# Gate and up of a SwiGLU by Strassen's seven products for four pairs of blocks, operands at low addresses

## The chip, the cores and the metric

The kernel runs on one core of a Trainium2 chip. The metric is the device time of one execution in microseconds (us). Its engines work at the same time and each takes its own instructions in the order in which they stand: PE (TensorE) multiplies matrices, DVE (VectorE) and ACT (ScalarE) work element by element, POOL (GpSimd) does a little arithmetic and issues DMAs, SP (SyncE) only issues DMAs. SBUF is the memory on the chip from which the engines read, PSUM the one into which PE accumulates, in eight banks of 128 x 512 float32 here.

## The reference

The program is a decoder trunk of two layers on `x` of 512 tokens by 1024 channels, all in float32:

```python
_, S, _ = x.shape          # 512 tokens, D_MODEL = 1024, D_FF = 2816
# layer 0: pooling mixer; layer 1: differential attention; after each mixer:
x = layernorm(ALPHA * x + mixer(x))
x = layernorm(ALPHA * x + swiglu(x))

def _swiglu(x, w_gate, w_up, w_down):
    return (jax.nn.silu(x @ w_gate) * (x @ w_up)) @ w_down
```

The change concerns the two SwiGLU blocks. Each has `gate` and `up`, 512 x 1024 by 1024 x 2816, and `down`, 512 x 2816 by 2816 x 1024.

## The kernel before

Every float32 operand of a product is held as two tiles of a matmul type: a high part, which an ACT cast makes, and a low part, which DVE makes by subtracting the high part from the original. A product is three matmuls, high by high, high by low and low by high (`mm3`, lines 106 to 110). The order on each engine is that of the program text; nothing reorders it.

**Gate and up.** The 2816 hidden columns are 22 blocks of 128 (`FB` = 22, `HALF` = 11). For each block and for each of gate and up there are 8 steps over the 1024 channels with 3 matmuls each, 24 matmuls of 128 x 128 weights by 512 tokens, into one PSUM bank. The first three blocks of layer 0 and the first two of layer 1 (`early`) are done in two halves of 256 tokens, since the second half of x comes later; the others run in the loop at lines 587 to 606. The blocks are taken in the order 0, 11, 1, 12, ..., so two consecutive ones form a pair k of hidden rows k and k+11. A weight tile of 128 x 1024 comes by a DMA on SP's queue (`raw`, four buffers, `RAWS`), is cast by ACT (line 89), and DVE makes the low part (line 90); there are six buffers for such pairs (`WBUFS`). After a block, ACT takes Silu of the gate (line 459) and DVE multiplies it with up (line 460), which gives a row of `hid`.

**Down** is already done by seven products in Winograd's form of Strassen's method, in the order P1, Q5, P6, Q3, P7, P2, Q4 (`DOWN`); each has 66 matmuls, 33 for each of two token blocks (line 629). What these products need as sums is made while gate and up run. `sum_weights` (line 474) loads four blocks of the weights of `down`, makes four sums on DVE (line 484) and stores them into DRAM (`tsum`) from POOL's queue. `sum_hidden` (line 491), after each pair of rows, makes sums of rows of `hid`: a copy of the first quarter to `a11` (ACT line 497, DVE line 499), three DVE operations of 256 columns (lines 498, 500 to 504), an ACT cast (line 505), and later the low part (line 508) and a store into `ssum`. While `down` runs, `r` tiles are loaded from the weights or from `tsum`, cast and subtracted (`dh`, `dl`), and the left operands come from `a11`, from `hid` or from `ssum`.

**Order around the change.** Six weights are prepared ahead. PE waits for a weight's low part and for its high part, ACT's cast waits for the DMA and for a free buffer, which PE frees when the product that used it is done. The affine part of the layer norm (lines 189, 190) and the loads of its parameters stand among the early blocks.

Of the kernel before, what the change touches and what calls it, by code (L numbers as in the profile page):

```python
# [50 lines left out]
def trunk(ctx, tc, x, wall, pscale, lam_p, subln, table, lng, lnb, band, first, onehot, out):  # L51
# [8 lines left out]

    res = keep.tile([P, SB, D], F32, name="res")
# [30 lines left out]
    def ready(upto, low=None):  # L92
        while divided[0] < min(upto, total):
            c = divided[0]
            fetch(c + RAWS)
            h = keep.tile([P, 1024], F32R, tag="wh", name=f"wh{c}", bufs=WBUFS)
            l = keep.tile([P, 1024], F32R, tag="wl", name=f"wl{c}", bufs=WBUFS)
            split(h, l, raws.pop(c), low=low)
            parts[c] = (h, l)
            divided[0] += 1  # L100
# [20 lines left out]


    xt = keep.tile([P, 2, 2, KB, 256], F32R, name="xt")
# [93 lines left out]
    with tc.tile_pool(name="pool", bufs=1) as pp:  # L217
# [52 lines left out]
        ph = pp.tile([P, KB, S], F32R, name="ph")  # L270
        pl = pp.tile([P, KB, S], F32R, name="pl")
# [13 lines left out]
        def pool_weights(c):  # L285
            h = keep.tile([P, 1024], F32R, tag="wh", name=f"pwh{c}", bufs=WBUFS)
            l = keep.tile([P, 1024], F32R, tag="wl", name=f"pwl{c}", bufs=WBUFS)
# [145 lines left out]

    ROWS = [slice(k, k + n) for k, n in PAIRS]

    def ffn(layer, late):
        n = 2 * layer + 1
        final = n == 2 * DEPTH - 1
        c0 = base[0]
        with tc.tile_pool(name=f"ffn{layer}", bufs=1) as fp:  # L440


            hid = fp.tile([P, FB, S], F32, name=f"hid{layer}")
            a11 = fp.tile([P, 2, HALF, 256], F32R, name=f"a11_{layer}")

            def product(acc, c, lo, hi):
                h, l = weights(c)
# [9 lines left out]
            def gated(f, pg, pu):  # L457
                sg = keep.tile([P, S], F32, tag="y", name=f"sg{layer}_{f}", bufs=2)
                nc.scalar.activation(sg, pg, AF.Silu)  # L459
                nc.vector.tensor_tensor(hid[:, f, :], sg, pu, op=ALU.mult)  # L460

            c1 = c0 + 2 * FB

            order = [k + j * HALF for k in range(HALF) for j in range(2)]
            tsum = dram.tile([4, len(PAIRS), P, 1024], F32, name=f"tsum{layer}")
            ssum = dram.tile([P, 2, 2, HALF, 256], F32, name=f"ssum{layer}")

            def block(i, b):

                if PAIRS[i][1] == 2:  # L470
                    return wall[c1 + 4 * i + b]
                return wall[c1 + 20 + b // 2][:, (b % 2) * 512 : (b % 2 + 1) * 512]

            def sum_weights(k):

                i, j = k // 2, k % 2
                c = slice(j * 512, (j + 1) * 512)
                b11, b12, b21, b22 = t = [
                    fp.tile([P, 512], F32, tag=f"b{b}", name=f"b{b}_{layer}_{k}") for b in range(4)
                ]  # L480
                for b in range(4):
                    nc.sync.dma_start(out=t[b], in_=block(i, b)[:, c])
                for z, x, y in ((b11, b11, b12), (b12, b12, b22), (b22, b11, b22), (b21, b22, b21)):
                    nc.vector.tensor_tensor(z, x, y, op=ALU.add)  # L484
                for m, z in enumerate((b11, b22, b12, b21)):
                    nc.gpsimd.dma_start(out=tsum[m, i, :, c], in_=z)

            late_low = []
            summed_rows = [0]

            def sum_hidden(k):
                first, second = hid[:, k, :256], hid[:, k, 256:]
                a12, a22 = hid[:, k + HALF, :256], hid[:, k + HALF, 256:]
                u = fp.tile([P, 2, 256], F32, tag="u", name=f"u{layer}_{k}", bufs=1)
                v = fp.tile([P, 2, 2, 256], F32R, tag="v", name=f"v{layer}_{k}", bufs=1)
                tt = nc.vector.tensor_tensor
# [16 lines left out]
            def settle():  # L513
                while late_low:
                    late_low.pop(0)()
# [587 lines left out]
```

## Time and profile before

Three runs took 980.78, 982.01 and 984.98 us, median 982.01 us.

| | us |
|---|---|
| profiled execution | 983.17 |
| its span in the trace | 981.1 |
| PE busy | 963.2 (98%) |
| DVE busy | 643.4 (66%) |
| ACT busy | 420.5 (43%) |
| POOL busy | 123.7 (13%) |

By stage, in us from the start of the span: pooling mixer 0 to 41, gate and up of layer 0 from 41 to 284, its down to 391, a turn to 406.6, attention to 570.5, its output product to 635, gate and up of layer 1 to 864, its down to 953.3, the tail to 981.1.

In rows of the page, "x66" counts instructions, "us, mean ns" are the busy time of a group and the duration of one. Matmuls overlap, so the time between the starts of two is less than a matmul's own duration. A row in a timeline is a start, a busy time and what ran, with "[idle <- engine]" for a wait ahead of it.

### The profile page before, as it was taken

The numbers are of one execution on the slowest core, as the hardware profiler recorded it, in microseconds if no ns is written. First come the engines' busy times: TensorE is split into PE (matmuls) and PEld (weight loads), VectorE is DVE, ScalarE is ACT, GpSimd is POOL, SyncE is SP. The second block draws the span as 40 slices with busy tenths as digits, with TensorE's granted clock in tenths as the row PEclk, the third lists the DMA queues.
The fourth block names the chain that finished last, engine by engine and source line by source line (L and its number), as shares of the span: only waits on it lengthen the run. The fifth ranks groups of instructions, "written<-read, shape, count | busy, mean of one in ns | idle before, by whom it ended". The sixth has DMA issues, their size and how long they took to land.

```text
span 981.1 us, 13416 instructions
## 1 busy us (share of the span) xinstructions
PE 963.2 (98%) x4974; PEld 820.6 (84%) x4974; DVE 643.4 (66%) x1007; ACT 420.5 (43%) x708; POOL 123.7 (13%) x195
## 2 busy tenths in 40 slices
PE   8999999999999999999999999999999999999995
PEld 8898888888888888988888888988888888888884
DVE  6845874455567577688777676756655555477687
ACT  5753222223326357656556554732223322244460
POOL 4201111111120211000000000011111111111102
PEclk9999999999999999999999999999999999999997
DMA  8247768655776984323222122276665566878942
GB/s 223 66 158 247 250 228 289 229 193 193 266 257 236 329 295 151 114 82 94 73 87 86 55 86 86 90 270 211 225 256 193 209 229 228 288 246 297 341 145 86
DMA packets 70079, 188.59 MB, mean 192 GB/s; under 512 B 15956, under 2 KB 16084, under 8 KB 70014
## 3 DMA queue, kind: packets, MB, share of 16 engines
q1 hardware_dynamic: 56588, 141.57, 42.1%
q0 software_dynamic: 13408, 46.15, 13.9%
q8 instruction: 39, 0.64, 0.3%
q14 instruction: 26, 0.21, 0.1%
q10 hardware_dynamic: 18, 0.02, 0.0%
HBM read 150.99 MB, written 36.72 MB: 191 GB/s over the span
## 4 chain that ended last, share of the span: by engine, by line
PE 94%; DVE 3%; ACT 1%; POOL 1%; issue 0%; POOLq 0%; DVEq 0%
PE P L629 13%; PE g L109 8%; PE u L108 8%; PE u L109 8%; PE g L108 8%; PE u L110 8%; PE g L110 8%; PE Q L629 6%; PE s L814 2%; PE v L108 2%; PE v L110 2%; PE v L109 2%; PE wo L108 2%; PE wo L109 2%; PE wo L110 2%; PE q L109 1%
## 5 line engine op out<-in xcount | busy, mean ns | idle before, releaser
L90 DVE TENSOR_TENSOR wl<-raw,wh 128x1024 fp32r<-128x1024 f32 x118 | 141.7, 1220 | 33.3 <-ACT wh L89 33.3
L89 ACT CAST wh<-raw 128x1024 fp32r<-128x1024 f32 x120 | 123.5, 1050 | 65.9 <-PE u L109 63.9
L109 PE MATMUL g<-xt,wh 128*128 128x512 f32 (+1 forms) x392 | 144.1, 368 | 0.5 <-DVE xt L90 0.5
L108 PE MATMUL g<-xt,wh 128*128 128x512 f32 (+1 forms) x392 | 144.3, 368 | 0.0
L108 PE MATMUL u<-xt,wh 128*128 128x512 f32 (+1 forms) x392 | 144.1, 368 | 0.0
L110 PE MATMUL u<-xt,wl 128*128 128x512 f32 (+1 forms) x392 | 144.0, 367 | 0.0
L109 PE MATMUL u<-xt,wh 128*128 128x512 f32 (+1 forms) x392 | 144.0, 367 | 0.0
L110 PE MATMUL g<-xt,wl 128*128 128x512 f32 (+1 forms) x392 | 144.0, 367 | 0.0
L460 DVE TENSOR_TENSOR hid<-sg,u 128x512 f32<-128x512 f32 x44 | 30.3, 688 | 154.9 <-PE u L110 154.5
L90 DVE TENSOR_TENSOR dl<-r,dh 128x1024 fp32r<-128x1024 f32 x84 | 94.3, 1132 | 38.8 <-ACT dh L89 38.7
L89 ACT CAST dh<-r 128x1024 fp32r<-128x1024 f32 x84 | 81.5, 979 | 69.6 <-PE P L629 31.7
L629 PE MATMUL P<-dh,xt 128*128 128x512 f32 x352 | 109.4, 390 | 0.0
L109 PEld LDWEIGHTS g<-xt,wh 128*128 128x128 f32 x392 | 73.9, 189 | 12.7 <-DVE xt L90 0.7
L110 PEld LDWEIGHTS u<-xt,wl 128*128 128x128 f32 x392 | 73.9, 189 | 12.3
L108 PEld LDWEIGHTS u<-xt,wh 128*128 128x128 f32 x392 | 73.9, 189 | 12.1
L110 PEld LDWEIGHTS g<-xt,wl 128*128 128x128 f32 x392 | 73.9, 188 | 12.2
L108 PEld LDWEIGHTS g<-xt,wh 128*128 128x128 f32 x392 | 73.9, 188 | 12.2
L109 PEld LDWEIGHTS u<-xt,wh 128*128 128x128 f32 x392 | 73.9, 188 | 12.0
L505 ACT CAST v<-u 128x512 fp32r<-128x512 f32 x22 | 13.7, 621 | 159.4 <-issue 142.5
L629 PEld LDWEIGHTS P<-dh,xt 128*128 128x128 f32 x352 | 66.1, 188 | 13.6
L484 DVE TENSOR_TENSOR b<-b,b 128x512 f32<-128x512 f32 x88 | 60.8, 691 | 18.4 <-DMA b<-in_wall 16.2
L459 ACT ACTIVATE sg<-g 128x512 f32<-128x512 f32 x44 | 26.3, 599 | 103.5 <-PE g L110 102.0
(189 smaller groups left out, 1792.5 us busy)
## 6 DMA issues: line engine op xcount, KB each, us to landing
raw<-in_wall SPq DMA_DIRECT2D x128, 512.0 KB, 4.2
b<-in_wall SPq DMA_DIRECT2D x88, 256.0 KB, 5.6
tsum<-b POOLq DMA_DIRECT2D x88, 256.0 KB, 4.7
r<-tsum SPq DMA_DIRECT2D x40, 512.0 KB, 4.7
r<-in_wall SPq DMA_DIRECT2D x30, 512.0 KB, 5.0
ssum<-v POOLq DMA_DIRECT2D x22, 512.0 KB, 4.0
xt<-ssum POOLq DMA_DIRECT2D x20, 512.0 KB, 6.0
res<-in_x SPq DMA_DIRECT2D x8, 256.0 KB, 6.4
```

The lines of the kernel that those rows point to most:

```text
L89: nc.scalar.copy(dst_h, src)
L90: (low or nc.vector).tensor_tensor(dst_l, src, dst_h.bitcast(F32), op=ALU.subtract)
L108: nc.tensor.matmul(acc, ah, bh, start=start, stop=False)
L109: nc.tensor.matmul(acc, ah, bl, start=False, stop=False)
L110: nc.tensor.matmul(acc, al, bh, start=False, stop=stop)
L459: nc.scalar.activation(sg, pg, AF.Silu)
L460: nc.vector.tensor_tensor(hid[:, f, :], sg, pu, op=ALU.mult)
L484: nc.vector.tensor_tensor(z, x, y, op=ALU.add)
L505: nc.scalar.copy(v[:, :, 0, :], u)
L629: nc.tensor.matmul(accs[s], x[:, k, r], y[:, c], start=first and k == 0 and e == 0, stop=last and k == m - 1 and e == 2, skip_group_check= ...
L814: nc.tensor.matmul(accs[c][:, :wide], a[r, qs], b[r, :wide], start=i == 0, stop=i == 2)
```

## The change

1. **Seven products for four pairs.** For the pairs 4, 6, 7 and 9 of hidden rows (`SPLIT`), in both layers, gate and up are done by `strassen(k)`: x is cut into two halves of tokens by two halves of channels, the weights into two halves of channels by gate and up. Each of the seven products has 24 matmuls of 128 x 128 by 256 tokens. Three PSUM banks are used: A (products P1, P6, P7, Q4), C (Q5, Q3) and B (P2). A and C go on accumulating after they have been copied out: A after P1 (ACT, line 814) and after P6 (line 818), C after Q5 (line 816); the others are taken out by DVE (lines 820, 822, 824), with two Silus (lines 825, 828) and two products on DVE (832, 834). Seven weight tiles are made out of four by four DVE sums of 128 x 1024 (line 552), then seven casts (line 555) and seven low parts (line 558) in place of four each. The weights are laid out for it beforehand.
2. **Sums of x** (`sums_of_x`): eight DVE operations, four casts and four low parts of 128 x 1024 per layer, spread over the early blocks and blocks 3 to 5.
3. **Weight sums of down**: a row's blocks come by two POOL DMAs, a third adds two blocks onto them while it transfers; DVE adds two times 128 x 512 (lines 657, 658) per row, and ACT's queue issues the two stores. The rows of sums stand at the early blocks 0 and 1, at blocks 3, 5, 7, 11 and 17, and behind each Strassen pair.
4. **`sum_hidden`** makes no `a11`; P1 of down gets its left operand from `hid`, and P6 a subtraction (line 719). `v` has two buffers, its store is issued by ACT.
5. **Placement**: the tiles of x, a region for pooled values, sums of x and attention heads, and the weight pairs are the first in SBUF, so that these operands have low addresses.
6. `RAWS` is 5; the scratch of dynamic DMAs is 8192 bytes; the loads of the norm's parameters stand elsewhere.

```diff
-RAWS = 4
+RAWS = 5
+SPLIT = (4, 6, 7, 9)
+GATE = ("P1", "Q5", "P6", "Q3", "P7", "P2", "Q4")
...
+    xt = keep.tile([P, 2, 2, KB, 256], F32R, name="xt")
+    def region(name):
+        return keep.tile([P, 8192], F32R, tag="region", name=name)
...
+                if k in SPLIT:
+                    chunks += [(c, ()), (c, (c, c + 1)), (c, (c, c + 2)), (c + 2, ())]
+                    chunks += [(c + 1, (c + 1, c + 2)), (c + 3, ()), (c, (c, c + 3))]
+                    step("cast", j0)
+                    for w in (
+                        "low 0, sum 1, cast 1, sum 4, cast 3, cast 4, low 1, sum 2, cast 2, low 3, "
+                        "low 2, sum 6, cast 5, cast 6, low 4, low 5, low 6"
+                    ).split(", "):
...
+                    if kind == "sum":
+                        tt(t, raws[pair[0]], raws[pair[1]], op=ALU.add)
+                    elif kind == "cast":
+                        halves[j] = weight_pair(f"g{layer}_{j}")
+                        nc.scalar.copy(halves[j][0], t)
+                    else:
+                        h, l = halves[j]
+                        tt(l, t, h.bitcast(F32), op=ALU.subtract)
...
+                for j in range(2):
+                    nc.gpsimd.dma_start(out=t[:, j], in_=src[:, j])
+                nc.gpsimd.dma_start(out=t[:, 0], in_=src[:, :, 1], accum_op=ALU.add)
...
+            def sum_terms(k):
+                t = terms.pop(k)
+                tt(t[:, 1, 1], t[:, 0, 0], t[:, 1, 1], op=ALU.add)
+                tt(t[:, 1, 0], t[:, 1, 1], t[:, 1, 0], op=ALU.add)
+                yield
...
+                for j in range(2):
+                    nc.scalar.dma_start(out=dst[:, j], in_=t[:, j])
...
             def sum_hidden(k):
...
-                nc.scalar.copy(a11[:, 0, k, :], first)
+                tt(u[:, 0, :], first, second, op=ALU.subtract)
                 tt(second, second, a22, op=ALU.subtract)
...
+                tt(u[:, 1, :], a12, first, op=ALU.subtract)
+                tt(u[:, 1, :], u[:, 1, :], second, op=ALU.add)
                 nc.scalar.copy(v[:, :, 0, :], u)
+                yield
+                tt(v[:, :, 1, :], u, v[:, :, 0, :].bitcast(F32), op=ALU.subtract)
+                yield
+                nc.scalar.dma_start(out=ssum[:, :, :, k, :], in_=v.bitcast(F32))
...
+            def strassen(k):
+                names = {"P1": "A", "P6": "A", "P7": "A", "Q4": "A", "Q5": "C", "Q3": "C", "P2": "B"}
...
+                for j, p in enumerate(GATE):
+                    acc = banks[names[p]]
+                    h, l = halves[index[k] + j]
+                    xh, xl = lefts[p]
+                    for f in range(2):
+                        o = acc[:, f * 256 : (f + 1) * 256]
+                        for kk in range(4):
+                            c = slice((4 * f + kk) * P, (4 * f + kk + 1) * P)
+                            for e, (w, x) in enumerate(((h, xh), (h, xl), (l, xh))):
+                                nc.tensor.matmul(
+                                    o, w[:, c], x[:, kk, :],
...
+                    if p == "P1":
+                        g0 = tile_of(0)
+                        nc.scalar.copy(both(g0), acc)
+                    elif p == "Q5":
+                        nc.scalar.copy(second, acc)
+                    elif p == "P6":
+                        nc.scalar.copy(first, acc)
+                    elif p == "Q3":
+                        tt(first, acc, first, op=ALU.subtract)
...
+                    ahead(index[k] + j + 6)
+                    catch_up()
...
+                weight_sums()
+                behind.append(sum_hidden(k))
```

`catch_up` runs the next piece of each unfinished `sum_terms` and `sum_hidden` (up to its next `yield`); `ahead` prepares weights up to the sixth product ahead.

The order on ACT in layer 0 between the blocks 13 and 16 (pairs 6 and 7), first before. The names `wh` and `g_..h` are high parts of weights, `sg` a Silu, `v` the sums of hidden rows, `a` the copy to a11.

```order
L459 ACTIVATE sg_17_1809<-g_13_1747 128x512
L497 CAST a_0_534<-hid_533 128x256
L505 CAST v_6_1813<-u_6_1812 128x2x256
L89 CAST wh_1849<-raw_1738 128x1024
L89 CAST wh_1897<-raw_1773 128x1024
L459 ACTIVATE sg_7_1901<-g_14_1821 128x512
L89 CAST wh_1932<-raw_1803 128x1024
```

The same place in the changed kernel: the second half of pair 6 is behind, pair 7 begins (A_7 and C_7 are its PSUM banks).

```order
L828 ACTIVATE sg_6_1_1961<-A_6_1727 128x512
L555 CAST g_39h<-raw_1804 128x1024
L555 CAST g_40h<-raw_1578 128x1024
L814 COPY sg_7_0_2001<-A_7_1974 128x512
L662 DMA tsum_536<-b_7_1612 128x2x512 x2
L687 CAST v_6_2013<-u_6_2012 128x2x256
L816 COPY hid_534<-C_7_1975 128x2x256
L555 CAST g_41h<-raw_1836 128x1024
L818 COPY hid_534<-A_7_1974 128x2x256
```

The copies out of the banks A_7 and C_7 stand in ACT's queue behind two stores and behind the cast of `v`, which was followed by weight casts alone before.

DVE at the same place, before; `wl` and `g_..l` are low parts of weights, `b` weight sums of down, `u` and `v` sums of hidden rows.

```order
L460 TENSOR_TENSOR hid_533<-sg_17_1809,u_13_1748 128x512
L498 TENSOR_TENSOR hid_533<-hid_533 128x256
L499 TENSOR_TENSOR a_0_534<-hid_533,a_0_534 128x256
L500 TENSOR_TENSOR hid_533<-hid_533 128x256
L501 SCALAR_TENSOR_TENSOR u_6_1812<-hid_533 128x256
L504 TENSOR_TENSOR u_6_1812<-hid_533 128x256
L90 TENSOR_TENSOR wl_1850<-raw_1738,wh_1849 128x1024
L508 TENSOR_TENSOR v_6_1813<-u_6_1812,v_6_1813 128x2x256
```

DVE in the changed kernel from P2 of pair 6 to the sums of its hidden rows:

```order
L824 TENSOR_TENSOR sg_6_0_1754<-B_6_1729,sg_6_0_1754 128x512
L832 TENSOR_TENSOR hid_534<-sg_6_0_1754,hid_534 128x2x256
L552 TENSOR_TENSOR raw_1578<-raw_1578,raw_1804 128x1024
L558 TENSOR_TENSOR g_38l<-raw_1694,g_38h 128x1024
L834 TENSOR_TENSOR hid_534<-sg_6_1_1961,hid_534 128x2x256
L657 TENSOR_TENSOR b_7_1612<-b_7_1612 128x512
L658 TENSOR_TENSOR b_7_1612<-b_7_1612 128x512
L558 TENSOR_TENSOR g_39l<-raw_1804,g_39h 128x1024
L683 TENSOR_TENSOR u_6_2012<-hid_534 128x256
L684 TENSOR_TENSOR hid_534<-hid_534 128x256
L685 TENSOR_TENSOR u_6_2012<-hid_534 128x256
L686 TENSOR_TENSOR u_6_2012<-u_6_2012,hid_534 128x256
```

Ahead of the rows of `u` there now stand weight sums, low parts and evacuations of PSUM of the pair itself, and the two weight sums of down.

More of the change, by code (lines that the diff above doesn't have):

```diff
@@ L459, in gated @@
                 nc.scalar.activation(sg, pg, AF.Silu)
[L460 to L486, printed above, removed]
@@ L609, in ffn @@
+            f = early
+            while f < FB:
+                if f // 2 in SPLIT:
+                    strassen(f // 2)
+                    f += 2
+                else:
+                    plain(f)
+                    f += 1
+            load_gb(n)
+            while behind:
+                catch_up()
             fetched[0] = divided[0] = c1 + FB
@@ L723, in scalars @@
                 )
+            whole = region("heads").rearrange("p (h i t) -> p h i t", h=HEADS, i=2)
+            slots = {h: whole[:, h] for h in range(HEADS)}
+            rest = xt[:, 1].rearrange("p i k t -> p (i k t)").rearrange("p (h i t) -> p h i t", h=4, i=2)
+            slots.update({16 + h: rest[:, h - 6] for h in (6, 7)})
             where = [base[0]]
```

350 lines of the change are left out of this document (251 added, 99 removed).

## The prediction

> **What bounds the kernel now.** I read the page's busy times and its chain of waits first, then the table of stretches, then the timeline of PE for the time from one matmul to the next.
>
> ```profile
> PE 963.2 (98%) x4974; PEld 820.6 (84%) x4974; DVE 643.4 (66%) x1007; ACT 420.5 (43%) x708; POOL 123.7 (13%) x195
> ...
> PE 94%; DVE 3%; ACT 1%; POOL 1%; issue 0%; POOLq 0%; DVEq 0%
> ```
>
> ```profile
> 41.00:284.00 243.00, 243.00 (x1216) 207.42 (x1217) 137.83 (x190) 78.16 (x114) 31.46 (x55) 1.00 0.66 225
> 284.00:391.00 107.00, 107.00 (x479) 88.10 (x477) 78.85 (x101) 58.40 (x85) 14.73 (x22) 1.00 0.73 253
> 635.00:864.00 229.00, 229.00 (x1055) 191.49 (x1054) 127.34 (x176) 64.39 (x86) 29.70 (x53) 1.00 0.67 234
> 864.00:953.30 89.30, 89.30 (x394) 73.66 (x393) 64.85 (x80) 46.04 (x59) 10.31 (x15) 1.00 0.76 268
> ```
>
> The columns are the stretch, its length, busy us of PE, weight loads, DVE, ACT and POOL, PE's granted clock, DMA share and GB/s. In gate and up and in down of both layers PE is busy for the whole stretch at clock 1.00, and it makes up 94% of the chain. So the time of these stretches is the number of matmuls by the time between their starts: taking matmuls away shortens it in full, and anything else counts only where it makes PE wait. DVE has 243.00 − 137.83 = 105 us free in the first gate and up, and 229.00 − 127.34 = 102 in the second; ACT has more.
>
> **Step 1, the matmuls.** Of the two shapes:
>
> ```profile
> 299.45 14.97 PE Q L629 x66
> ```
>
> ```profile
> 41.97 0.28 PE L108 MATMUL g<-xt,wh 128*128 128x256 f32 x1
> ...
> 44.97 0.28 PE L109 MATMUL u<-xt,wh 128*128 128x256 f32 x1
> ```
>
> The first row, of the chain, is one product of down: 66 matmuls of 512 columns in 14.97 us, 226.8 ns each. The other two, of PE's timeline, have 24 rows between them: 25 matmuls of 256 columns in 44.97 − 41.97 = 3.00 us, 120.0 ns each. A pair of blocks was 4 x 24 = 96 matmuls of 512: 96 x 226.8 = 21.77 us. It becomes 7 x 24 = 168 of 256: 168 x 120.0 = 20.16 us, 2.88 per product. That is −1.61 a pair and −12.9 for the eight pairs. One multiplication in eight goes (12.5%), but only 7.4% of the time, since two matmuls of 256 columns take 13 ns more than one of 512.
>
> By the Trainium skill ("TensorE: Matmul & The Clock Gate", section "Back-to-back issue gap") a lone matmul costs columns / 2.4 GHz plus about 2.5 ns, 215.8 and 109.2 ns, by which this step would be an estimated −19.0 us. The same section gives 81 ns at 128 and 131 ns at 512 columns as what is sustained between matmuls that each load weights; between these, 256 columns come to about 98 ns, and the step would be an estimated +31 us, a loss. The rows decide against both, as this trace has both shapes, each with a weight load per matmul.
>
> **Step 2, the addresses.** Two places of the trace are slower per matmul of 512 columns than the rest:
>
> ```profile
> 284.10 15.35 PE P L629 x66
> ...
> 863.72 15.35 PE P L629 x66
> 879.07 14.97 PE Q L629 x66
> ```
>
> ```profile
> 595.78 0.39 PE L109 MATMUL wo<-wl,oh 128*128 128x512 f32 x1
> ...
> 598.12 0.39 PE L110 MATMUL wo<-wh,ol 128*128 128x512 f32 x1
> ```
>
> P1 of down takes 15.35 us in both layers, 0.38 more than Q5: 232.6 ns a matmul. Attention's output product takes (598.12 − 595.78) / 10 = 234 ns (nine rows lie between). The first reads `a11`, the second `oh` and `ol`; both tiles lie at the high end of SBUF in the program before, and the change puts their replacements low. If it is the address, the gain is 2 x 0.38 = 0.8 us for P1 and 192 x (234 − 227) = 1.3 for the 192 matmuls of that product, of which those of heads 6 and 7 read a third tile: I take −1.9 in all. Bounds: 0 (it is something else) and −2.1. The Trainium skill ("SBUF — State Buffer", section "Who interferes with whom") has PE wait for no one, which makes this part nothing; the 0.38 us of the rows above speaks for some cost of place, and whether it is the place only the run tells.
>
> **Step 3, the new waits.** The copies out of PSUM are in the order of ACT's queue, and PE has one product (2.88 us) between the end of Q5 and the start of Q3, which goes on accumulating in C. Line 816 must be done by then. It stands behind the cast of `v`, which needs the four DVE operations of 256 columns of the hidden sums, and these stand behind whatever DVE is late with. The prices:
>
> ```profile
> L90 DVE TENSOR_TENSOR wl<-raw,wh 128x1024 fp32r<-128x1024 f32 x118 | 141.7, 1220 | 33.3 <-ACT wh L89 33.3
> L460 DVE TENSOR_TENSOR hid<-sg,u 128x512 f32<-128x512 f32 x44 | 30.3, 688 | 154.9 <-PE u L110 154.5
> L616 DVE SCALAR_TENSOR_TENSOR res<-res,P 128x512 f32<-128x512 f32 x20 | 13.4, 682 | 3.2 <-PE P L629 3.2
> L498 DVE TENSOR_TENSOR hid<-hid 128x256 f32<-128x256 f32 x22 | 9.3, 424 | 0.7
> ```
>
> ```profile
> L89 ACT CAST wh<-raw 128x1024 fp32r<-128x1024 f32 x120 | 123.5, 1050 | 65.9 <-PE u L109 63.9 <-issue 1.3 <-ACT line L422 0.7
> L505 ACT CAST v<-u 128x512 fp32r<-128x512 f32 x22 | 13.7, 621 | 159.4 <-issue 142.5 <-DVE u L504 16.9
> L89 ACT CAST kh<-k 128x512 fp32r<-128x512 f32 x8 | 4.7, 587 | 26.1 <-PE k L110 26.1
> ```
>
> ```profile
> 104.84 2.35 DVE L90 TENSOR_TENSOR wl<-raw,wh 128x1024 fp32r<-128x1024 f32 x2
> 110.12 0.69 DVE L460 TENSOR_TENSOR hid<-sg,u 128x512 f32<-128x512 f32 x1 [2.93 <-PE u L110]
> 110.84 0.42 DVE L498 TENSOR_TENSOR hid<-hid 128x256 f32<-128x256 f32 x1
> ...
> 112.78 1.22 DVE L189 TENSOR_TENSOR res<-res,gb 128x1024 f32<-128x1024 f32 x1
> ```
>
> ```profile
> 109.85 0.39 PE L108 MATMUL g<-xt,wh 128*128 128x512 f32 x1
> ```
>
> Neighbours overlap a little: two of 1024 columns take 2.35 (so the second adds 1.13), five of 256 take 112.78 − 110.84 = 1.94, 0.39 each. From the first matmul of the next product (109.85) to DVE's start on the finished bank (110.12) pass 0.27 us.
>
> A pair that follows plain blocks (4, 6, 9; t = 0 is its first matmul): DVE starts the last Silu product at 0.27 and has it, two weight sums, one weight sum of 1024 and a low part done by 4.5. ACT copies A at 3.15 to 3.75 and casts a weight to 4.8, whose low part ends at 5.95. The four operations of `u` end at 7.6, the cast of `v` at 8.25, the copy of C at 8.85. Q3 is due at 3 x 2.88 = 8.64: PE waits about 0.25.
>
> Pair 7 follows pair 6 directly. DVE begins line 820 of pair 6 after Q3, at 4 x 2.88 + 0.25 + 0.27 = 12.05. From there to the end of the four operations of `u` stand nine of 1024 columns (1.13 to 1.22: 10.2 to 11.0 us), seven of 512 (0.60 to 0.69: 4.2 to 4.8), four of 256 (1.6) and a Silu between lines 824 and 832 that DVE waits for (0.60 and two hand-overs, 0.75): 16.8 to 18.2, so 28.9 to 30.2. The cast of `v` and the copy of C with their hand-overs are 1.4 more: 30.3 to 31.6. Q3 of pair 7 is due at 20.16 + 0.25 + 8.64 = 29.05. PE waits 1.2 to 2.6 us; I take 2.0, as most of these operations need the one before. That DVE has no pause between 12 and 30 us, though the stage as a whole has 100 us free, is the point: the free time lies in other pairs.
>
> Per layer 3 x 0.25 + 2.0 = 2.75, both layers +5.5. Bounds: 0 (no copy is late: hand-overs and prices all at their low end), and 2.6 in all eight pairs, +21, if each starts as late as pair 7.
>
> **What I cost at nothing.** The added DVE work per layer is 4 x 3 = 12 more low parts, 16 weight sums, 12 operations on x (40 x 1.13 = 45 us) and evacuations, against the 102 to 105 us free; without that cover it would be those 45 us. Weights stay up to six products (17 us) ahead, against 4.2 us for a load and 2.3 for cast and low part. The casts added are under half of ACT's free time. Moved DMAs:
>
> ```profile
> raw<-in_wall SPq DMA_DIRECT2D x128, 512.0 KB, 4.2
> b<-in_wall SPq DMA_DIRECT2D x88, 256.0 KB, 5.6
> tsum<-b POOLq DMA_DIRECT2D x88, 256.0 KB, 4.7
> ```
>
> SP loses the 88 loads of `b`, POOL the 88 stores and 22 of `v`, which ACT now issues. A row of weight sums comes by two loads and a third transfer on top of them; at the prices of the rows of `b` and `tsum` that is some 16 us if they go one after the other (5.6 + 5.6 + 4.7). They are issued two rows ahead, some 40 us, and for row 3 one row, 21.8 us (step 1). If the sum waited, DVE would stand at line 657 with the low parts of the next weights behind it, and PE behind those. The low parts added to P1 of down and the subtraction added to P6 cost DVE six operations of 512 columns in each, in stretches with 107.00 − 78.85 = 28 and 24 us free. Head and tail have the same instructions.
>
> **The sum.** −12.9 − 1.9 + 5.5 = −9.3 us on the profiled execution's own time, 983.17 (span 981.1 and 2.1 around it): 973.9. That execution lies 1.2 above the median of the runs, 982.0, on which the sum gives 972.7. I forecast 973.3.
>
> **The rivals.**
>
> *All waits hidden.* The copies come in time: for it, three of four pairs per layer are only 0.25 us over by hand, and two neighbours on DVE can overlap more than I take. Against it, pair 7's sum is over even at its low end. −12.9 − 1.9 = −14.8: 967.8.
>
> *The waits eat the gain.* DVE is the bound of a Strassen pair. A pair has 11 operations of 1024 columns (12.4 to 13.4 us), seven of 512 and the low part of `v` (4.8 to 5.5), four of 256 (1.6) and the Silu (0.75): 19.6 to 21.3 against PE's 20.16. Against it, six of eight pairs come after plain blocks of 10.9 us in which DVE has a third free. If each pair runs 1.2 to 1.6 us over, 8 x 1.4 = 11.2 instead of 5.5: 982.0 − 14.8 + 11.2 = 978.4, and with 0 for the addresses 980.3. About 980, no change.
>
> *A late chain of three transfers, slower.* POOL's accumulating transfer reads what the first wrote, its speed is in no row, and DVE waits for it in its queue at line 657. Up to 21.8 us for the three it costs nothing; from about there DVE starts its sums late behind every Strassen pair, and pair 7's upper price comes up in all eight: 8 x 2.6 = 21, 982.0 − 14.8 + 21 = 988. For it speaks that the copies stand behind it on ACT too; against it that 16 us are not 21.8, and that the DMA share is 0.67.
>
> *The change does not do what it says.* The addresses might do nothing, +1.9 on the forecast, 975.2; it stays inside the forecast's own range.
>
> **How the numbers follow.** The forecast, with part of the waits, .45; waits hidden .25; gain eaten .20; slower .10. Half a percent, 4.9 us, is about what such runs tell from no change: faster is below 977.1. The forecast's own range is 970 to 977, of which I leave .05 above. Faster: .40 + .25 + .05 of the eaten gain = .70. Same: .05 + .14 = .19, and .01 from the edge of the slower case, .20. Slower: .10. The range takes the hidden case from 966.5 and the eaten one up to 982: below it lie .05, above it .12.
>
> **What would show it.** The row of 66 for P1 of down at 14.97 (step 2). 168 matmuls of 256 columns in 20.2 us in pair 4 (step 1). Waits of PE ahead of Q3, at line 816's copy, about 0.25 in pairs 4, 6, 9 and 2.0 in pair 7 (step 3), and none elsewhere in gate and up. What would make it wrong: a spacing of 256 columns other than 120 ns with the new weights, waits for low parts instead of copies, or DVE at line 657 waiting for a DMA.

## The result and the profile after

The change took 970.01 us, median of six runs (967.32 to 971.13), against 981.89 us of the kernel before in the same sessions. The ratio is 0.9875, 95% interval 0.9854 to 0.9895: 1.25% faster, where 973.3 us and 0.9% were forecast. The profiled execution took 971.13 us, its span 969.2.

The first lines of the page of the change, busy time and the chain that ended last:

```profile
PE 950.4 (98%) x5550; PEld 838.2 (86%) x5550; DVE 722.7 (75%) x1069; ACT 462.6 (48%) x754; POOL 120.5 (12%) x151
...
PE 89%; DVE 7%; ACT 2%; issue 1%; POOL 1%; POOLq 0%; DVEq 0%; ACTq 0%
```

DVE now has 7% of the chain instead of 3%. Where it stands is seen by stage. In the next two fences the span is cut at the same places in both kernels: at the first matmul of gate and up, of down, of attention, of attention's output product, of the next gate and up and of the next down, and at the end of the last matmul. The stage of attention is left out. The columns are the stretch, its length, busy time of PE, weight loads, DVE, ACT and POOL, then PE's granted clock, DMA share and GB/s. These cuts differ from those ahead of the prediction: gate and up of layer 1 begins at 621.96 us and not at 635, and its down runs to the last matmul at 968.84. The kernel before:

```profile
40.14:283.94 243.80, 243.31 (x1219) 207.52 (x1217) 138.48 (x192) 78.98 (x116) 31.98 (x55) 1.00 0.66 225
283.94:392.26 108.32, 108.07 (x487) 89.01 (x486) 80.17 (x103) 59.66 (x86) 14.75 (x22) 1.00 0.72 250
...
570.49:621.96 51.47, 51.47 (x245) 41.97 (x243) 38.58 (x67) 25.21 (x52) 3.85 (x7) 1.00 0.25 81
621.96:863.56 241.60, 241.60 (x1164) 204.15 (x1163) 135.90 (x187) 76.80 (x110) 30.32 (x54) 1.00 0.65 227
863.56:968.84 105.28, 105.28 (x463) 86.58 (x461) 79.67 (x104) 48.21 (x63) 15.12 (x22) 1.00 0.67 237
968.84:981.10 12.26, 0.00 (x0) 0.00 (x0) 6.05 (x10) 0.00 (x0) 2.43 (x3) 0.59 0.23 86
```

The change:

```profile
40.17:279.63 239.46, 237.68 (x1506) 216.27 (x1505) 176.56 (x217) 99.46 (x137) 32.33 (x37) 1.00 0.78 249
279.63:387.40 107.77, 107.56 (x488) 89.06 (x486) 82.16 (x108) 60.10 (x88) 12.55 (x18) 1.00 0.72 245
...
565.55:616.56 51.01, 50.80 (x245) 41.92 (x243) 38.58 (x67) 25.18 (x52) 3.84 (x7) 1.00 0.25 83
616.56:853.87 237.31, 236.02 (x1451) 212.94 (x1450) 173.90 (x212) 97.15 (x131) 30.40 (x35) 1.00 0.78 245
853.87:958.75 104.88, 104.88 (x463) 86.55 (x461) 82.09 (x109) 49.02 (x65) 13.06 (x18) 1.00 0.66 231
958.75:969.20 10.45, 0.00 (x1) 0.00 (x0) 6.06 (x10) 0.00 (x0) 2.44 (x3) 0.59 0.27 100
```

| stage | before | after | difference, us |
|---|---|---|---|
| gate and up, layer 0 | 243.80 | 239.46 | −4.34 |
| down and turn, layer 0 | 108.32 | 107.77 | −0.55 |
| attention's output product and turn | 51.47 | 51.01 | −0.46 |
| gate and up, layer 1 | 241.60 | 237.31 | −4.29 |
| down, layer 1 | 105.28 | 104.88 | −0.40 |
| after the last matmul | 12.26 | 10.45 | −1.81 |

With the first stage the same to 0.03 and attention 0.08 shorter this is the whole of 981.1 − 969.2 = 11.9. The last row was in no term of the prediction.

PE's waits for ACT's copy of bank C, in the view of waits (total us, number, longest):

```profile
PE C L805 <- ACT hid L816: 2.6, 2, 1.3
```

Two waits, one per layer. Both are ahead of Q3 of pair 7, as the timelines of DVE, ACT and PE show for layer 0 (start, duration; pair 6 ends at 194.04):

```profile
185.67 0.69 DVE L820 TENSOR_TENSOR hid<-C,hid 128x512 f32<-128x512 f32 x1 [1.09 <-PE C L805]
...
198.80 0.69 DVE L657 TENSOR_TENSOR b<-b 128x512 f32<-128x512 f32 x1
...
202.51 0.42 DVE L686 TENSOR_TENSOR u<-u,hid 128x256 f32<-128x256 f32 x1
```

```profile
202.97 0.62 ACT L687 CAST v<-u 128x512 fp32r<-128x512 f32 x1 [4.18 <-DVE u L686]
203.50 0.58 ACT L816 COPY hid<-C 128x512 f32<-128x512 f32 x1
```

```profile
204.13 0.39 PE L805 MATMUL C<-xs,g_37h 128*128 128x256 f32 x1 [1.29 <-ACT hid L816]
```

From line 820 to the end of line 686 DVE works for 202.93 − 185.67 = 17.3 us with one pause of 0.70 us for a Silu; the cast of v, the copy and Q3 follow one after the other. Q3's first matmul starts 1.57 us behind the matmul before it instead of 0.12, so PE loses 1.45 us; 1.29 us of them are counted as idle time. Ahead of the cast ACT is idle for 4.18 us: it isn't short of time, it stands in its queue. In pair 4, which follows plain blocks, the same copy comes just in time:

```profile
139.70 0.58 ACT L816 COPY hid<-C 128x512 f32<-128x512 f32 x1
```

```profile
140.14 0.28 PE L805 MATMUL A<-xs,g_18l 128*128 128x256 f32 x1
140.33 0.50 PE L805 MATMUL C<-xs,g_19h 128*128 128x256 f32 x2
```

The copy ends at 140.28, and Q3 starts 0.19 instead of 0.12 us behind the matmul before it. P1 of down is as fast as the other products:

```profile
854.03 14.96 PE P L870 x66
868.99 14.96 PE Q L870 x66
```

### The profile page after: what moved, and what is told of

It reads as the page before. It is cut to its first block, busy times and chain, and to the rows that moved or that the text cites. A ratio compares the mean times of both kernels' runs of the same rounds, so it can differ in the third digit from the quotient of the medians.

```text
span 969.2 us, 14409 instructions
## 1 busy us (share of the span) xinstructions
PE 950.4 (98%) x5550; PEld 838.2 (86%) x5550; DVE 722.7 (75%) x1069; ACT 462.6 (48%) x754; POOL 120.5 (12%) x151
## 3 DMA queue, kind: packets, MB, share of 16 engines
q1 hardware_dynamic: 43052, 115.35, 35.2%
## 4 chain that ended last, share of the span: by engine, by line
PE 89%; DVE 7%; ACT 2%; issue 1%; POOL 1%; POOLq 0%; DVEq 0%; ACTq 0%
PE P L870 13%; PE A L805 7%; PE Q L870 6%; PE g L126 5%; PE u L127 5%; PE g L127 5%; PE u L125 5%; PE u L126 5%; PE g L125 5%; PE C L805 4%; PE s L1060 2%; PE B L805 2%; PE v L125 2%; PE v L126 2%; PE v L127 2%; PE q L126 1%
## 5 line engine op out<-in xcount | busy, mean ns | idle before, releaser
L107 ACT CAST xs<-hid 128x512 fp32r<-128x512 f32 (+1 forms) x60 | 34.7, 581 | 23.0 <-DVE hid L719 23.0
L108 DVE TENSOR_TENSOR xs<-hid,xs 128x512 fp32r<-128x512 f32 (+1 forms) x60 | 38.4, 641 | 7.8 <-ACT xs L107 7.8
L217 ACT ACTIVATE y<-pt,bT,gT 128x128 f32<-128x128 f32 x96 | 36.0, 455 | 16.8 <-PE pt L212 15.8
L1070 ACT ACTIVATE p<-p,mn 128x128 f32<-128x128 f32 (+3 forms) x64 | 35.4, 553 | 14.9 <-DVE mn L1065 14.9
L552 DVE TENSOR_TENSOR raw<-raw,raw 128x1024 f32<-128x1024 f32 x32 | 39.1, 1220 | 0.3
L651 POOL DMA_DIRECT2D hid<-in_wall x24 | 18.8, 827 | 91.6 <-DMA tsum<-hid 46.1
L1065 DVE CUSTOM_DVE_ANT_0 p<-s,bias 128x128 f32<-128x128 f32 (+3 forms) x64 | 28.1, 485 | 0.0
L166 DVE BATCH_NORM_STATS2 st<-res 128x6 f32<-128x512 f32 x32 | 22.2, 695 | 1.1
L652 POOL DMA_DIRECT2D hid<-in_wall x12 | 14.8, 1232 | 54.7 <-DMA hid<-in_wall 49.4
L1084 DVE SCALAR_TENSOR_TENSOR p<-p,sm,p 128x128 f32<-128x128 f32 (+3 forms) x32 | 17.6, 551 | 1.1
L1060 PE MATMUL s<-heads 64*128 64x256 f32 (+2 forms) x192 | 17.9, 330 | 0.0
```

The source lines that it names most:

```text
L107: nc.scalar.copy(dst_h, src)
L108: (low or nc.vector).tensor_tensor(dst_l, src, dst_h.bitcast(F32), op=ALU.subtract)
L217: nc.scalar.activation(y[:, k, :], pt[:, k * P : (k + 1) * P], AF.Identity, bias=bT[:, n, kk : kk + 1], scale=gT[:, n, kk : kk + 1],)
L552: tt(t, raws[pair[0]], raws[pair[1]], op=ALU.add)
L651: nc.gpsimd.dma_start(out=t[:, j], in_=src[:, j])
L1060: nc.tensor.matmul(accs[c][:, :wide], a[r, qs], b[r, :wide], start=i == 0, stop=i == 2)
```

## The experiments

Theory: the matmuls give 12.9 us; PE loses part of it ahead of Q3 of pair 7, since the copy of bank C stands in ACT's queue behind the cast of v, and that behind DVE's backlog from pair 6; the addresses give something over 1 us. The rivals were that DVE itself is the bound of a pair, that ACT's stores hold the copy, and, for P1, that a11's layout made it slow and not its high address. The length of the first stage differs from one execution to the next (last section), so kernels are compared by the length of the stages; where a ratio is given, it is to runs of the kernel before in the same session.

**e1: the copy first.**

```diff
                     ahead(index[k] + j + 6)
-                    catch_up()
+                    if p != "P1":
+                        catch_up()
```

> In each Strassen pair the operations of the last hidden sums and the cast of v are issued one product later, so that the copy of bank C (line 816) stands in ACT's queue ahead of the cast of v. Theory (the copy waits in ACT's queue for v, and v for DVE's backlog): PE's wait ahead of Q3 in pair 7, 1.45 us in each layer, goes, and with it most of the 0.15 us by which the other pairs are over 20.16; about 969.2 - 2.9 = 966.3 for the span of the profile. Rival (DVE's backlog itself is the bound, and the wait comes back at the next thing that DVE or ACT owes, as the copy of bank A after P6 or a low part): the wait of 1.45 moves to P7, Q4 or the next blocks, and the span stays at 969. Second rival (ACT is late by itself, by the stores it issues): the same as the rival.

963.93 us, ratio 0.9824 (0.9807 to 0.9841). Its two gate and up stages:

```profile
36.52:273.96 237.44, 236.95 (x1506) 216.13 (x1505) 176.19 (x217) 99.62 (x137) 32.34 (x37) 1.00 0.77 247
610.87:846.15 235.28, 235.28 (x1452) 212.75 (x1450) 173.53 (x212) 97.46 (x131) 30.39 (x35) 1.00 0.78 246
```

They are 2.02 and 2.03 us shorter than in the change, and 6.36 and 6.32 shorter than before, against 6.45 for four pairs without any wait. PE's waits no longer have a row for a copy. The wait was made by the order of the cast and the copy in ACT's queue and came back nowhere; for four pairs the rivals that DVE is the bound or that ACT is late by itself fall. The rest of the fall in span (7.8 us) is the first stage, 36.52 against 40.17 us.

**e2: no neighbours.**

```diff
-SPLIT = (4, 6, 7, 9)
+SPLIT = (3, 5, 7, 9)
...
-                if f in (3, 5, 7, 11, 17):
+                if f in (3, 5, 9, 13, 17):
```

> The pairs 3, 5, 7 and 9 are split instead of 4, 6, 7 and 9, and the weight sums of down stand behind blocks 3, 5, 9, 13 and 17, so that no Strassen pair follows another; the number of matmuls is the same. Theory (pair 7 waits since pair 6 leaves DVE behind): no wait over 0.2 us ahead of any Q3, span 969.2 - 2.9 = 966.3. Rival (the queue order alone makes it, whatever DVE has behind it): waits of the order of 1.4 us in all or some pairs, span 969 or more. Pair 3 starts right behind the sums of x; if these are late, a new wait stands at its Q5.

978.23 us, ratio 0.9981 (0.9968 to 0.9994), slower than the change. The view of waits:

```profile
PE C L805 <- ACT hid L816: 8.4, 2, 6.2
PE A L805 <- DVE xs L603: 0.5, 1, 0.5
```

Pairs 5, 7 and 9 take 20.31 us each, so none of them loses more than 0.15 us, as the theory has it. But in pair 3 PE waits for 6.2 us in layer 0 and 2.2 in layer 1, at the same copy. Here the backlog is that of the early blocks: sums of x, layer norm and the sums of hidden rows keep DVE without a pause from 91.4 us on, and the cast of v comes at 120.54:

```profile
120.08 0.42 DVE L686 TENSOR_TENSOR u<-u,hid 128x256 f32<-128x256 f32 x1
```

The wait costs more than its own length, since PE's granted clock is at half behind it:

```profile
122.00:126.00 4.00, 4.00 (x20) 4.00 (x20) 1.47 (x2) 2.02 (x3) 1.46 (x2) 0.50 1.02 372
```

At 0.50 the matmuls of 256 columns start 0.21 us apart instead of 0.12, and Q3 takes 5.05 us instead of 2.88; in layer 1, behind the shorter wait, it takes 4.46. Gate and up take 247.16 and 239.78 us in all. I had expected at most a late Q5, and a gain in all. The mechanism holds with another source of backlog; the forecast of the time missed.

**e3: no pair split.**

```diff
-SPLIT = (4, 6, 7, 9)
+SPLIT = ()
...
-                if f in (3, 5, 7, 11, 17):
+                if f in (3, 5, 7, 9, 11, 13, 15, 17, 19):
```

> No pair is split: gate and up are plain in all blocks, everything else of the change stays (placement, sums of x though nothing uses them, three transfers per row of weight sums, sums behind every odd block from 3 to 19). Theory: gate and up take 243.8 and 241.6 us again (239.6 and 237.5 in the change), so span 969.2 + 8.6 = 977.8; P1 of down stays at 14.96. If the end of the program (1.8 us shorter in the change behind the last store) belongs to the rest of the change it stays at 26.05 us after the last product, if it is chance or belongs to the splitting it goes back towards 27.9 and the span is 979.6. Rival (the lighter rest of the change freed PE too): less than 8.6 of difference.

976.70 us, ratio 0.9955 (0.9939 to 0.9971).

```profile
38.85:282.62 243.77, 243.28 (x1218) 207.55 (x1217) 135.72 (x177) 81.39 (x113) 32.31 (x37) 1.00 0.77 247
619.52:861.13 241.61, 241.61 (x1163) 204.28 (x1162) 133.09 (x172) 79.25 (x107) 30.39 (x35) 1.00 0.76 245
```

Gate and up are those of the kernel before to 0.03 us, so splitting, with its waits, is worth 8.6 us and nothing else of the change alters the length of these stages. P1 stays at 14.96, and 10.39 us pass after the last matmul: both belong to the rest of the change.

**e11: two weight sums moved.** Behind pair 6 the sums of lines 657 and 658 are left out and made behind block 10.

```diff
-                if f in (3, 5, 7, 11, 17):
+                if f in (3, 5, 7, 10, 11, 17):
...
-                weight_sums()
+                if k != 6:
+                    weight_sums()
```

> The change with one thing moved: the two weight sums of down (lines 657 and 658) that stand behind pair 6 stand behind block 10. Theory (the copy of C of pair 7 is late by what DVE still owes): these two take 1.33 us on DVE (198.80 to 200.13 in the change), so the wait ahead of Q3 of pair 7 falls from 1.45 to about 0.1 us in both layers. Rival (ACT's stores ahead of the cast of v, lines 662, hold the copy): these two stores go from that place too, but their issue takes 0.37 us each while ACT is idle; if they were the cause the wait would fall by 0.7 us or less, to 0.7.

One run, 968.58 us. The waits at the copy:

```profile
PE C L805 <- ACT hid L816: 0.2, 1, 0.2
```

PE's loss ahead of Q3 of pair 7 falls from 1.45 to 0.38 and 0.12 us, gate and up to 238.41 and 235.98 us, 1.05 and 1.33 less than in the change. 1.33 us of DVE work taken away give 1.05 to 1.33 us: the wait is DVE's backlog. The two stores that ACT issues went from this place too, but they were put at 0.7 us at most, and the loss fell by 1.07 and 1.33.

**e5: six pairs.** The order of e1 and

```diff
-SPLIT = (4, 6, 7, 9)
+SPLIT = (4, 5, 6, 7, 8, 9)
...
-                if f in (3, 5, 7, 11, 17):
+                if f in (3, 5, 7):
```

> The order of e1 (copy of bank C ahead of the cast of v) with six pairs split, 4 to 9, all neighbours; weight sums of down behind blocks 3, 5, 7 and each pair. A pair without waits saves 1.60 us, so two pairs more in two layers are worth 4 x 1.60 = 6.4 us. If DVE keeps up over six pairs in a row (19.6 to 21.3 us of DVE work per pair by the prediction's count, about 19.9 by the timeline of pair 6 in the change, against PE's 20.16): gate and up of a layer take 237.45 - 3.2 = 234.2 us, 6.4 us under e1. If DVE is the bound of a pair: new waits of up to 1 us per pair from the third neighbour on, gate and up 236 to 239.

957.72 us, ratio 0.9771 (0.9751 to 0.9792): with e9 the fastest, some 10 us under the change by the two ratios (0.9875 − 0.9771, of 982 us).

```profile
38.56:272.76 234.20, 233.71 (x1651) 220.37 (x1649) 195.61 (x237) 108.61 (x149) 32.38 (x37) 1.00 0.81 253
609.73:841.75 232.02, 232.02 (x1595) 217.01 (x1594) 192.93 (x232) 106.52 (x143) 30.43 (x35) 1.00 0.81 252
```

3.2 us less than e1 in each layer, as forecast, without a wait. DVE keeps up over six neighbours once its lateness doesn't stand in the way of a copy.

**e10: seven pairs**, e5 with pair 10 too and weight sums behind blocks 3 and 5. In this kernel a copy of pair 9 overwrites part of the weight sums of row 8 before they are stored, so these sums are not those of the reference; the instructions and their order are those meant.

> e5 with seven pairs split, 4 to 10, weight sums of down behind blocks 3, 5 and each pair. Two pairs more in all, 2 x 1.60 = 3.2 us less than e5 if DVE keeps up (gate and up 232.6 and 230.4 us); if the end of gate and up, where the first weights of down are prepared, gets short of DVE, a new wait of 1 to 3 us at P1 of down.

971.21 us, ratio 0.9909 (0.9887 to 0.9931), some 13 us more than e5, where 3.2 us less or at worst 1 to 3 us more had been expected.

```profile
PE A L805 <- ACT hid L818: 4.8, 2, 2.4
PE P L871 <- ACT xs L107: 3.4, 3, 1.4
```

PE now waits in pair 9 and in the first products of down; down of layer 0 takes 114.40 us in place of 107.8. What ACT and DVE wait for there, by the views of their own waits:

```profile
ACT hid L818 <- DMA tsum<-hid: 5.5, 2, 2.8
DVE b L657 <- DMA b<-in_wall: 2.5, 1, 2.5
```

In pair 9 the copy after P6 waits for the stores of the weight sums of row 8, which lie in rows of `hid` that pair 9 itself writes. Behind pair 10, in layer 0, DVE waits for the loads of the last weight sums until 279.23 us, and ACT's cast of v and its next casts for down stand behind that. So both delays begin with a DMA. This kernel does not show that DVE is the bound at seven pairs; whether it could keep up stays open.

**e4, e7, e8, e12: the addresses.** In e4 the region is allocated in the pool of each stage, so that it lies at 185664 in the SwiGLU stages and not at 41088:

```diff
-    def region(name):
-        return keep.tile([P, 8192], F32R, tag="region", name=name)
+    def region(name, pool):
+        return pool.tile([P, 8192], F32R, tag="region", name=name)
```

> The region (pooled values, sums of x, left operands of down, attention heads) is allocated in each stage's own pool at the high end: the left operands of down at 185664 and up in place of 41088, the heads at 156544 and up; nothing else changes in the order of work. Theory (the address sets the 15.35 against 14.96 us): all seven products of down become slower by up to 0.39 us each, 14 x 0.39 = 5.5 us in all, and the output product of attention goes from 227 back to 231 to 238 ns per matmul; the Strassen products that read sums of x (Q5, P6, P7, Q3) become slower too; span 974 to 976. Rival (a11's own layout or neighbours made P1 slow, not the address): products of down stay at 14.96, span 969.

967.69 us, ratio 0.9861 (0.9842 to 0.9880); products of down take 15.11 us, attention's output product 50.98 as in the change. So this place costs something in down, less than a11's had cost, and nothing in attention. I had expected up to 0.39 us for each product, and it is 0.15; I had expected 974 to 976 us and slower Strassen products from the region, and they became faster, 2.74 us instead of 2.88, so that all eight copies of C are now late:

```profile
PE C L805 <- ACT hid L816: 4.7, 8, 1.8
```

Two kernels separate height from distance: e7 is e4 with a pad that puts the region a multiple of 4096 bytes from the weight pairs; e8 is the change with the region low but 832 bytes off. Both have four raw tiles for space. One run each, 967.76 and 967.53 us.

```diff
+            pad = fp.tile([P, 720], F32, name=f"pad{layer}")
             xs = region(f"xs{layer}", fp)
```

```diff
+    pad = keep.tile([P, 304], F32, name="pad")
     pooled = region("pooled").rearrange("p (i k t) -> p i k t", i=2, k=KB)
     ph, pl = pooled[:, 0], pooled[:, 1]
+    pad2 = keep.tile([P, 208], F32, name="pad2")
```

> e4 (region high) with a pad, so that the region is a multiple of 4096 bytes from the weight pairs, as in the change (four raw tiles, for space). In e4 the Strassen products whose moving operand lies in the region took 114 ns per matmul (120 from x), and the products of down whose stationary operand lies there 15.11 us (14.96 in the change). If the distance modulo 4096 decides: 120 ns and 14.96 again. If the height decides: 114 ns and 15.11 as in e4.

> The change with the region low, at 42304, but off from the weight pairs by 832 bytes modulo 2048 (pads before and behind it; four raw tiles for space). If the distance decides: 114 ns in the products that read the region, 15.1 us in down. If the height decides: 120 ns and 14.96 as in the change.

A product of down in e7 and in e8:

```profile
850.68 14.96 PE P L872 x66
```

```profile
849.54 15.11 PE P L874 x66
```

and a Strassen product from the region in e8, 24 matmuls from the first to the third row:

```profile
131.05 0.40 PE L809 MATMUL C<-xs,g_17h 128*128 128x256 f32 x2
...
133.79 0.28 PE L809 MATMUL A<-xs,g_18h 128*128 128x256 f32 x1
```

The region high and aligned behaves as low and aligned; low and off behaves as high and off: 2.74 us for 24 matmuls, 114 ns each. It is the distance, not the height. e12 asks the same of a11 itself, in the kernel before:

```diff
+            pad = fp.tile([P, 416], F32, name=f"pad{layer}")
             a11 = fp.tile([P, 2, HALF, 256], F32R, name=f"a11_{layer}")
```

> The kernel before with a pad of 1664 bytes ahead of a11, so that a11 moves up from 189760 to 191424, still at the high end, but a multiple of 2048 from the weight pairs (384 off that before); nothing else. If the distance between the two operands sets P1's 15.35 us: 14.97 in both layers, 0.77 us in all. If the height or a11's layout does: 15.35.

```profile
859.82 14.96 PE P L631 x66
```

1664 bytes higher, P1 takes 14.96 us (one run, 978.62 us). So it was the distance there too, and not a11's layout.

**e6: the scratch alone**, in the kernel before.

```diff
-    nc = bacc.Bacc("TRN2", target_bir_lowering=False, num_devices=1)
+    nc = bacc.Bacc(
+        "TRN2", target_bir_lowering=False, num_devices=1, dynamic_dma_scratch_size=8192
+    )
```

> The kernel before with the scratch of dynamic DMAs at 8192 bytes, nothing else; all tiles move down by 8192 bytes, a11 from 189760 to 181568. From the last matmul to the end of the span: 12.26 us in the kernel before, 10.28 to 10.45 in all kernels with the change. If the scratch makes it: 10.4, and the span 979.3. If the rest of the change makes it (who issues the DMAs): 12.3. P1 of down: 15.35 if a11's distance from the other operands modulo 4096 or the like makes it slow, 14.96 if an address above some 185000 does.

978.93 us, ratio 0.9989 (0.9977 to 1.0000). After the last matmul:

```profile
965.83:976.00 10.17, 0.00 (x1) 0.00 (x0) 6.07 (x10) 0.00 (x0) 2.44 (x3) 0.70 0.27 103
```

10.17 instead of 12.26 us, with the same DVE and POOL work. e12, which keeps the default, has 12.17. The scratch makes the end of the program shorter by about 2 us. The trace shows where: POOL's queue ends with three instructions named DRAIN, and the longest of them (in ns, the last of the three figures) takes 6.78 us in the kernel before, first row, and 2.78 in e6, second row:

```profile
L1099 POOLq DRAIN  x3: 40/102/6780, 973.5 to 980.8; - x3
L1099 POOLq DRAIN  x3: 40/102/2778, 970.5 to 975.8; - x3
```

It is 6.78 us in e12 too, and 2.77 or 2.78 in every kernel with 8192 bytes. Of these 4.0 us about 2 count, since SP's queue then ends last. Why the DRAIN depends on the scratch is not shown. P1 stays at 15.35 with a11 8192 bytes lower, in line with the distance.

**e9: six pairs, x and region off the weights.** e5 with the tiles `ident`, `gT`, `bT` and a pad of 64 bytes put between the region and the weight pairs, 832 bytes in all:

```diff
+    ident = keep.tile([P, P], F32, name="ident")
+    gT = keep.tile([P, 2 * DEPTH, KB], F32, name="gT")
+    bT = keep.tile([P, 2 * DEPTH, KB], F32, name="bT")
+    pad = keep.tile([P, 16], F32, name="pad")
     first_pair = weight_pair("pw0")
```

> e5 (six pairs, copy of C first) with x and the region off from the weight pairs by 832 bytes (1216 modulo 2048, the distance at which e4 and e8 had 114 ns); nothing else. By the distance: all seven products of a pair at 24 x 114 = 2.74 us, a pair 19.2 instead of 20.16 us, twelve pairs 12 us less; the early blocks of 256 columns 0.14 a product less, 20 products in two layers, 3 us less; down 0.96 us more in each layer (15.11 per product); the plain blocks of 512 columns with x moving are unknown, between 227 and 220 ns. But DVE has 19.9 us of work per pair by the timeline of pair 6, so from the second neighbour on waits of about 0.7 us per pair come up: 5 pairs x 0.7 x 2 layers = 7 us back. Net -6 us against e5, gate and up of a layer 230 to 232 us. If x gains nothing from the distance and only the region does (four of seven products): -3 us or none.

957.77 us, ratio 0.9777 (0.9755 to 0.9800), the same as e5, not 6 us less. One of its stretches, a pair long, and its plain blocks:

```profile
183.97:204.02 20.05, 19.32 (x171) 19.13 (x170) 19.18 (x24) 10.24 (x13) 2.20 (x3) 1.00 0.78 238
```

```profile
76.03 0.40 PE L131 MATMUL g<-xt,g_6h 128*128 128x512 f32 x1
...
77.20 0.39 PE L130 MATMUL u<-xt,g_7h 128*128 128x512 f32 x1
```

The matmuls of a pair would take 7 x 2.72 = 19.04 us, but a pair takes 20.05: DVE is busy for 19.18 and waits 0.70 for a Silu, and the rest are pauses of under 0.05 us between its instructions. DVE is the bound of a pair here, and the lateness comes up ten times at the copy of A after P6 (line 820 in this kernel):

```profile
PE A L807 <- ACT hid L820: 7.1, 10, 0.7
```

Matmuls of 512 columns with x off take (77.20 − 76.03) / 5 = 234 ns instead of 227, which I had left open. Gate and up are 1.3 and 0.3 us shorter than in e5; down (0.95 and 1.05 us longer) and attention (0.74 longer) take that back.

## Why the prediction was right, point by point

- **Step 1, the matmuls (−12.9).** 24 matmuls of 256 columns take 2.88 us in the change, and with the waits gone (e1) the two stages are 6.36 and 6.32 us shorter: −12.7. The times of the Trainium skill ("TensorE: Matmul & The Clock Gate", section "Back-to-back issue gap") would have given an estimated −19 or +31; −12.7 agrees with neither.
- **Step 2, the addresses (−1.9).** P1 fell from 15.35 to 14.96 us in both layers, −0.78, as forecast. Attention's output product gave −0.46, not −1.1 to −1.3: that term was mis-sized. By PE's timeline its matmuls went from 233.4 ns apart to 228.2 and not to 227 (the mean without gaps over 300 ns), which is 1.0 us for 192; in the middle of the stage the transposes now start 0.36 us later behind them, as PE waits for DVE, and this takes part of it back. The reason I gave, a high address, is wrong: e7, e8 and e12 show that the distance to the other operand decides. By the Trainium skill ("SBUF — State Buffer", section "Who interferes with whom") PE never waits for another engine at SBUF; these runs don't speak against that, since both operands are PE's own.
- **Step 3, the waits (+5.5).** The mechanism, the place and the order in which things are late were as worked out: DVE's run of 17.3 us against 16.8 to 18.2, PE's wait 1.45 against 1.2 to 2.6, of which I took 2.0. Pairs 4, 6 and 9 take 20.31 us by PE's timeline, 0.15 over 20.16, against 0.25. e1 puts all of it at 4.05 us against 5.5. This is the largest miss among the terms, 1.5 us too much.
- **Costed at nothing.** e3 shows gate and up without splitting at 243.77 and 241.61, so sums of x and moved DMAs cost nothing there. They are not free in every place: in e2, where they stand right ahead of a Strassen pair, PE waits for 6.2 us.
- **What the sum lacked.** The end of the program, −1.81, of which e6 shows the scratch as the cause. I had put the tail at nothing because its instructions are the same, and had passed over that part of the diff.

The terms measured are −12.7 + 4.05 − 1.2 − 1.8 = −11.7, and −0.2 in small pieces of down and attention. The forecast's −9.3 lies 1.5 us short by the waits and 1.8 by the end, and 0.7 too far by the addresses. On the median the sum gave 972.7, and 973.3 was forecast; 970.01 lies at the very edge of the forecast's own range of 970 to 977. The direction and the mechanism were right; that the time still lies inside that range, with 1.8 us from a term that the sum lacked, is luck. The rival that the waits are all hidden, 967.8, ended nearer to 970.0 than the forecast, but not by its mechanism: the waits were there, and the shorter end of the program made up for part of them.

The rival of DVE as the bound of every pair has its place too: DVE needs 20.05 us per pair in e9, just under the 20.16 that PE's matmuls take in the change. That fits e5, which runs six pairs without a wait, and e9, where faster matmuls shorten a pair by only 0.1 us.

## What to carry to other kernels

When a product is traded for sums, read the engine that makes the sums at the place, not over the stage: DVE had 60 us free in the stage and worked for 17 us almost without a pause in one spot. Where PE waits for a copy out of PSUM, put that copy ahead of anything in its queue that depends on a late engine; letting the copy go first was worth 4 us here, and with that order two more pairs ran without a wait. Look at the granted clock behind a longer wait of PE: in e2 it fell to half, and the matmuls behind the wait were slow as well. Before crediting an address, move one operand by a kilobyte or so and leave its height as it is.

## What the runs showed of the hardware that I had not expected

**Distance between operands.** With the tiles of the two operands a multiple of 2048 bytes apart, matmuls of 256 and 512 columns start 120.0 and 226.7 ns apart. With the moving operand 1216 bytes off modulo 2048 it is 113.3 and 233 ns (e9; 114 ns in e8, where the region moved and not the weights, so that neither tile's own address decides), with the stationary operand off by the same, 229 on average (15.11 us for 66), and with a11's 384 it was 232.6. Not each distance costs: attention's output product in e4 has its heads 768 off and takes 50.98 us as in the change. What the rule is, I can't say.

**The end of the program** is some 2 us shorter with a smaller scratch for dynamic DMAs, by POOL's last DRAIN of 2.78 us instead of 6.78 (e6).

**The first stage** took between 35.2 and 40.2 us in profiles whose instructions there are nearly the same. In the profile of before and in that of e1, matmuls of 256 columns at 13 us:

```profile
13.09 0.41 PE L313 MATMUL pool<-fh,xt 128*128 128x256 f32 x1
13.31 0.41 PE L311 MATMUL pool<-fh,xt 128*128 128x256 f32 x1
```

```profile
13.00 0.28 PE L327 MATMUL pool<-bh,xt 128*128 128x256 f32 x1
13.11 0.29 PE L326 MATMUL pool<-bh,xt 128*128 128x256 f32 x1
```

0.21 us apart in the one, 0.12 in the other, while the view gives a granted clock of 1.00 for both. But the records of the clock begin only at 18.6 us in the traces of before and of the change, and at 6.7 us in that of e1; where there is none, the view shows 1.00. In e5 there is one, and matmuls of 256 columns are 0.21 us apart in this stretch, as in e2 at 0.50:

```profile
9.00:15.00 6.00, 6.00 (x23) 4.92 (x23) 3.68 (x6) 3.71 (x7) 1.78 (x2) 0.50 1.05 344
```

So the longer spacing in before and in the change is most likely this half clock, too, though their traces have no record of it. The Trainium skill ("TensorE: Matmul & The Clock Gate", section "What you observe") has matmuls at the start of a run take almost twice as long until some 4 us of sustained activity have passed; the two spacings, 0.21 and 0.12 us, agree with the ratio, and these runs do not show the 4 us. The profiles of before and of the change both have the longer spacing, so their difference holds; in e1, e2, e4, e6 to e10 and e12 the stage is 3.4 to 5.0 us shorter than in these two, in e3 and e5 1.3 to 1.6.
